# One grid for all the chains of a mixer: writing TensorE's order out by hand

## The chip, the core and the metric

The kernel runs on one core of a Trainium2 chip. The metric is device time in microseconds (us) of one execution; a few executions are timed and their median is given. The profile is one execution on the same core, taken apart by engine: PE (TensorE, matrix products), DVE (VectorE), ACT (ScalarE), POOL (GpSimd) and SP (the queue that issues the weight loads).

## The reference, cut to what matters

A decoder layer on 256 rows of 2048 columns, all in float32:

```
x = LN1(alpha*x + 0.5*swiglu(x, gate1, up1, down1))
p = x @ w_in                                  # 2048 x 6432
o_attn = diff_attention(p[:, :3072])          # 8 heads, two softmaxes each, causal, ALiBi
o_rwkv = rwkv7(p[:, 3072:])                   # 16 heads of 64, delta-rule state, decay, gate
x = LN2(alpha*x + concat(o_attn, o_rwkv) @ w_out)
x = LN3(alpha*x + 0.5*swiglu(x, gate2, up2, down2))
```

The change touches only the two middle products and what lies between them, the mixer. In rwkv7 a state of 64 x 64 per head runs over the rows; `k` is normalised, `r`, `k` and two products of `k` are scaled by cumulated decays, and a gate closes the output.

## The kernel before, in words

**Products.** Every large product is formed from three rounded terms. A pair of weight tiles (256 rows x 512 columns) is loaded by SP into `raw`; ACT rounds it into `wh` (L143), DVE subtracts to get the rest `wl` (L146), and PE adds `wh*xh`, `wl*xh` and `wh*xl` (L153 to L155). The 256 rows of x are two halves of 128 (`tt` 0 and 1). One *step* is one pair of weight tiles: six products for the first half of the rows, and six for the second half with the pair of two steps earlier, so twelve products of 128 x 512. The rounded halves have five slots in this phase (`NW["mix"]`), so ACT can round a new pair only when PE is through with the pair five steps before it.

**Chains.** Between the products stand chains of small operations. `chan_major` turns the finished block of `p` by PE transposes (`tr`, L584), ACT or DVE copies it to `praw`, and `shift` mixes each of its four parts with the previous row: ACT writes `df` (L590), DVE writes the result (L596). `df` has one buffer. `rwkv_group` makes the decays (L731), normalises `k` (Square L746, a product with `bones` L753), scales, and forms `Q` by products masked on DVE (L789, L792); a loop of 31 steps on DVE inverts the triangles of 32 x 32; then the state runs over four blocks (L890 to L930), and two norms and the gate follow (L945 to L980). `rwkv_values` turns `v` (L701) and forms the bonus (L713). `attn_heads` does two heads at a time. There are two groups of everything: rwkv group 0 and 1 (each eight heads), attention group 0 and 1 (each four heads).

**Who sets the order.** Each chain is a Python generator; `Stream.run_bg` is called after each pair of weight tiles and moves the chains on. Up to the last block of `w_in` they advance by credit: each `yield` names a cost, each step grants 1.6 (`BG`) or 0.5 (`AT`), and the order of all engines' instructions is afterwards set by the scheduler of the tile framework, which also moves PE's small matrix products to where it thinks their inputs are ready. The output product `w_out` has three parts: part 0 (attention group 0 and rwkv group 0, 16 steps), part 1 (attention group 1, 8 steps), part 2 (rwkv group 1, 8 steps). In parts 0 and 1 PE's order is written out by hand (`manual_schedule`): PE executes what the program emits, in that order, and each chain moves one `yield` per step. Before a part starts, `ready` drains the chains that it needs and splits their outputs (`split`, L89 and L90). PSUM banks of the chains: `sm` has two, `pr` one, `at` two, shared with `tr`.

Of the kernel before, what the change touches and what calls it, by code (L numbers as in the profile page):

```python
# [16 lines left out]
P = 128  # L17
# [18 lines left out]
BG = 1.6  # L36
AT = 0.5


def build(tc, A, out):  # L40
# [58 lines left out]
    class Stream:  # L99
        def __init__(self):  # L100
            self.pend = []
            self.tail = []
            self.roles = None
            self.behind = []
            self.acc = {}
            self.bg = []
            self.credit = {}
            self.hooks = {}
            self.step = 0
            self.slot = 0  # L110
            self.even = False
            self.hold = {}

# [157 lines left out]
        def flush(self, lag=0):  # L271
# [9 lines left out]
            while self.pend:  # L281
                self.mm(self.pend.pop(0), 1)

        def spawn(self, gen, rate):
            self.bg.append(gen)
            self.credit[gen] = [0.0, rate]

        def run_bg(self):
            if self.even:
                for g in list(self.bg):  # L290
                    if self.hold.get(g):
                        self.hold[g] -= 1
                        continue
                    while g in self.bg:
                        try:
                            if next(g) != 0:
                                break
                        except StopIteration:
                            self.bg.remove(g)
                return  # L300
            for g in list(self.bg):
                c = self.credit[g]
                c[0] = min(c[0], 0.0) + c[1]
                while c[0] > 0 and g in self.bg:
                    try:
                        cost = next(g)
                    except StopIteration:
                        self.bg.remove(g)
                        break
                    if cost is None:  # L310
                        break
                    c[0] -= cost
# [246 lines left out]
    def mix(mp, pq, C):  # L559
# [17 lines left out]
        def chan_major(acc, tt, widths, dst):  # L577
# [3 lines left out]
            tr = bank("tr", (P, 4, P))  # L581
            o = 0
            for i, w in enumerate(widths):
                T.transpose(tr[:w, i, :], tm[:, o:o + w], ident)  # L584
                o += w
            dst(tr)
# [12 lines left out]
        def lora_done(tt, acc):  # L599
            if tt == 0:  # L600
                pr = hp.tile([P, 4, S + 1], F32, tag="J1", name=nm("praw"))
                V.memset(pr[:, :, 0:1], 0.0)
                lora["raw"] = pr
            pr = lora["raw"]

            def dst(tr):
                c = slice(1 + tt * P, 1 + (tt + 1) * P)
# [3 lines left out]
            chan_major(acc, tt, [P, P, 32], dst)  # L611
            if tt == 1:
# [12 lines left out]
                lora.update(tw=tw, g1=g1, g2=g2)  # L625

# [20 lines left out]
        def rwkv_start(g, prev=None):  # L647
# [5 lines left out]
            stream.spawn(st["gen"], BG)  # L653
            return st

        def rwkv_cols(g, st, parts):
            gr = st["group"]

            def done(tt, acc, i):
                if tt == 0:  # L660
                    pr = hp.tile([P, 4, S + 1], F32, tag="J1" if g == 0 and i == 2 else "H3", name=nm("praw"))
                    V.memset(pr[:, :, 0:1], 0.0)
                    st["raw"] = pr
                pr = st["raw"]
                chan_major(acc, tt, [P] * 4, lambda tr: SC.copy(out=pr[:, :, 1 + tt * P:1 + (tt + 1) * P], in_=tr))
                if tt == 1:
# [4 lines left out]
                    if i == 2:  # L671
                        st["gen2"] = rwkv_values(g, st)
                        stream.spawn(st["gen2"], BG)
# [17 lines left out]
        def rwkv_values(g, st):  # L691
            prev = st["prev"]
            while "rk" not in st or (prev is not None and "chain" not in prev):
                yield None
            vp, vv, rk = st["group"].vp, st["group"].vv, st["rk"]
            SV = hp.tile([P, 4, 4, 2, 64], F32, tag="J1", name=nm("SV"))
            st["SV"] = SV
            for p in range(4):
                ps = bank("pr", (P, 4, P))
# [4 lines left out]
                yield 0.3  # L704
# [3 lines left out]
            SC.copy(out=SV[0:64, :, 3, 1, :], in_=ps[0:64, :, 64:128])  # L708
            yield 0.3
            for hf in range(2):  # L710
                ps = bank("pr", (P, 2, S))
# [3 lines left out]
                yield 0.6  # L715
            st["values"] = True

        def rwkv_group(g, st):
# [7 lines left out]
            for hf in range(2):  # L726
                for k in range(2):
                    ps = bank("pr", (P, 2, S))
                    for i in range(2):
                        c0 = (2 * hf + i) * P  # L730
                        T.matmul(ps[:, i, :], wa[:, c0:c0 + P], lora["tw"][:, k, :], start=True, stop=True)  # L731
                    for i in range(2):
                        p = 2 * hf + i
                        o, x = (tl[:, p, :], ps[:, i, :]) if k == 0 else (av[:, p], ps[:, i, :].rearrange("p (c t) -> p c t", c=4))
                        SC.activation(out=o, in_=x, func=AF.Sigmoid, bias=col(k, g, p))
                    yield 0.6
# [13 lines left out]
            for hf in range(2):  # L750
                ps = bank("pr", (P, 2, S))
# [3 lines left out]
                yield 0.6  # L755
# [38 lines left out]
            rk = t4("lw")  # L794
            for p in range(4):
                V.scalar_tensor_tensor(out=v4(rk)[:, p], in0=rh[:, p], scalar=col(4, g, p), in1=ka[:, p], op0=ALU.mult, op1=ALU.mult)
            st["rk"] = rk
            yield 1.5

            def transposed():  # L800
# [5 lines left out]
                for h in range(2):  # L806
                    for e in range(2):
                        r = slice(64 * e, 64 * e + 64)
                        ps = bank("sm", (P, 8, 64))
                        for i in range(8):  # L810
                            T.transpose(ps[:, i, :], BK[r, 2 * h + i // 4, i % 4, e:e + 2].rearrange("p a t -> p (a t)"), ident[r, r])
                        for p in range(2):
                            SC.copy(out=bt[2 * h + p][:, :, e, :], in_=ps[:, 4 * p:4 * p + 4])
# [28 lines left out]
            while "values" not in st or (g == 1 and "over" not in lora):  # L842
                st["wait"] = True
                yield None
            SV = st["SV"]
# [9 lines left out]
            if g == 1:  # L855
                yield from transposed()
# [19 lines left out]
            yield 0.6  # L876
            if g == 0:
                yield from transposed()
            BT = st["bt"]
            st["cols"] = True  # L880
# [4 lines left out]
            for c in range(4):  # L885
# [6 lines left out]
                V.tensor_copy(out=Rs, in_=ps)  # L892
                yield 0.6
# [6 lines left out]
                SC.copy(out=SV[64:128, :, c, 1, :], in_=ps[64:128])  # L900
                yield 0.6
                if c < 3:
# [14 lines left out]
                    yield 0.6 * (1 - g)  # L917
# [23 lines left out]
            for hf in range(2):  # L941
# [5 lines left out]
                yield 0.6 * (1 - g * (1 - hf))  # L947
# [3 lines left out]
            for hf in range(2):  # L951
# [5 lines left out]
                yield 0.6 * (1 - g * (1 - hf))  # L957
            SC.activation(out=merge(nrm), in_=merge(nrm), func=AF.Exp, scale=-0.5)
            yield 0.6 * (1 - g)
            V.tensor_tensor(out=merge(Yc), in0=merge(Yc), in1=merge(nrm), op=ALU.mult)  # L960
            yield 0.6 * (1 - g)
            for p in range(4):
                V.tensor_scalar(out=Yc[:, p], in0=Yc[:, p], scalar1=col(5, g, p), scalar2=col(6, g, p), op0=ALU.mult, op1=ALU.add)
            yield 0.6 * (1 - g)
            V.tensor_tensor(out=sq, in0=Yc, in1=v4(vv), op=ALU.add)
            yield 0.6 * (1 - g)
            st["gate"] = True
            while g == 0 and "v" not in st.get("next", ()):
                yield None
# [278 lines left out]
```

## Time and profile before

| | us |
|---|---|
| median of 3 runs | 1916.03 (1914.43 to 1919.23) |
| profiled execution, its own time | 1915.6 |
| its span | 1913.8 |
| PE busy | 1883.6 (98%) |
| DVE busy | 1624.6 (85%) |
| ACT busy | 1095.3 (57%) |
| mean granted PE clock | 0.995 |

The page gives busy time per engine, and rows by line; a row of the timeline has start, duration, engine, line and operation, and in brackets how long the engine had been idle before it and who released it. PE's products overlap one another in the records, so the distance of their starts counts, not their durations. A small fp32 product that is no transpose leaves two records (64 instructions at L862, 128 records). The mixer lies between about 700 and 1221 us: the first products with `w_in` overlap the end of LN1, `w_out` starts at 1078 us, and LN2 ends it.

### The profile page before, as it was taken

Reading aid. Unit: us, or ns where it says so; the run is one execution under the profiler, and the core shown is the slowest. Engines: PE = TensorE matmul, PEld = TensorE weight load, DVE = VectorE, ACT = ScalarE, POOL = GpSimd, SP = SyncE. Lnnn points to the kernel's source line nnn. Section 1 sums busy time; section 2 is a strip of 40 time slices with the busy share of each in tenths; the row PEclk is TensorE's granted clock in tenths of the full one; section 3 lists DMA queues with packets and bytes.
Section 4 is the critical chain, followed back from the end, with each engine's and each line's share of the span. In section 5 each row is a group of like instructions: output and inputs, shape, how many; then the busy total and the mean of one; then the engine's idle time right before and its main releaser. Section 6 shows DMA issues by size and latency. Waiting matters only on the chain.

```text
span 1913.8 us, 24938 instructions
## 1 busy us (share of the span) xinstructions
PE 1883.6 (98%) x9335; PEld 1549.8 (81%) x9335; DVE 1624.6 (85%) x1834; ACT 1095.3 (57%) x1376; POOL 72.6 (4%) x110
## 2 busy tenths in 40 slices
PE   9999999999999999999999999999999999999997
PEld 7888888888888888887778778788888888888886
DVE  8999987789999976777678777999999778999996
ACT  6656665556666536656555544566666545666651
POOL 0000101100000000000000000000000110000000
PEclk9999999999999999999999999999999999999999
DMA  9766676766667456555445545776666676666743
GB/s 312 247 198 218 186 239 217 233 212 199 217 216 233 142 173 198 163 160 154 146 117 159 162 148 194 260 246 198 199 211 227 213 236 213 197 210 213 228 153 131
DMA packets 207320, 381.72 MB, mean 199 GB/s; under 512 B 23530, under 2 KB 25648, under 8 KB 206944
## 3 DMA queue, kind: packets, MB, share of 16 engines
q1 hardware_dynamic: 182928, 350.53, 56.5%
q0 software_dynamic: 6832, 15.32, 2.9%
q10 hardware_dynamic: 17440, 14.29, 2.6%
q8 instruction: 73, 1.20, 0.3%
q14 instruction: 47, 0.39, 0.1%
HBM read 368.29 MB, written 11.80 MB: 199 GB/s over the span
## 4 chain that ended last, share of the span: by engine, by line
PE 59%; DVE 2%; issue 1%; ACT 1%; DMA 0%; ACTq 0%; DVEq 0%
PE acc L153 18%; PE acc L154 18%; PE acc L155 18%; PE sm L789 1%; DVE wl L146 1%; PE tr L584 0%; PE tr L443 0%; PE at L1027 0%; DVE y L345 0%; PE pr L731 0%; DVE y L353 0%; PE sm L890 0%; PE sm L898 0%; DMA dY<-Y 0%; PE sm L923 0%
## 5 line engine op out<-in xcount | busy, mean ns | idle before, releaser
L143 ACT CAST wh<-raw 128x1024 fp32r<-128x1024 f32 (+2 forms) x833 | 853.7, 1049 | 604.5 <-PE acc L155 377.8
L146 DVE TENSOR_TENSOR wl<-raw,wh 128x1024 fp32r<-128x1024 f32 (+2 forms) x833 | 984.5, 1215 | 207.1 <-ACT wh L143 202.7
L154 PE MATMUL acc<-wl,xh 128*128 128x512 f32 (+1 forms) x1552 | 606.2, 392 | 1.9 <-DVE wl L146 1.9
L155 PE MATMUL acc<-wh,xl 128*128 128x512 f32 (+1 forms) x1552 | 604.8, 391 | 1.0 <-DVE xl L90 1.0
L153 PE MATMUL acc<-wh,xh 128*128 128x512 f32 (+1 forms) x1552 | 600.0, 394 | 5.2 <-ACT xh L89 3.3
L153 PEld LDWEIGHTS acc<-wh,xh 128*128 128x128 f32 x1552 | 292.7, 189 | 67.2 <-ACT xh L89 4.9
L155 PEld LDWEIGHTS acc<-wh,xl 128*128 128x128 f32 x1552 | 292.9, 189 | 61.6 <-DVE xl L90 1.7
L154 PEld LDWEIGHTS acc<-wl,xh 128*128 128x128 f32 x1552 | 292.8, 189 | 61.7 <-DVE wl L146 3.5
L224 DVE TENSOR_TENSOR raw<-raw,raw 128x2048 f32<-128x2048 f32 x112 | 256.0, 2286 | 1.1 <-DMA raw<-in_ffn_w_gate_dram 0.5
L154 PE MATMUL acc<-wl,hh 128*128 128x512 f32 x544 | 212.0, 390 | 0.0
L155 PE MATMUL acc<-wh,hh 128*128 128x512 f32 x544 | 211.4, 389 | 0.0
L153 PE MATMUL acc<-wh,hh 128*128 128x512 f32 x544 | 210.9, 390 | 0.0
L153 PE MATMUL acc<-wh,s 128*128 128x512 f32 x448 | 174.9, 390 | 1.0 <-ACT acc L250 1.0
L155 PE MATMUL acc<-wh,s 128*128 128x512 f32 x448 | 174.6, 390 | 0.0
L154 PE MATMUL acc<-wl,s 128*128 128x512 f32 x448 | 174.3, 389 | 0.0
L153 PEld LDWEIGHTS acc<-wh,hh 128*128 128x128 f32 x544 | 102.1, 188 | 21.8 <-ACT wh L143 0.4
L155 PEld LDWEIGHTS acc<-wh,hh 128*128 128x128 f32 x544 | 102.1, 188 | 21.1
L154 PEld LDWEIGHTS acc<-wl,hh 128*128 128x128 f32 x544 | 102.2, 188 | 20.9
L153 PEld LDWEIGHTS acc<-wh,s 128*128 128x128 f32 x448 | 84.1, 188 | 19.1 <-ACT acc L250 1.5
L154 PEld LDWEIGHTS acc<-wl,s 128*128 128x128 f32 x448 | 84.1, 188 | 17.4
L155 PEld LDWEIGHTS acc<-wh,s 128*128 128x128 f32 x448 | 84.1, 188 | 17.4
L237 ACT COPY acc<-acc 128x512 f32<-128x512 f32 x28 | 16.0, 572 | 51.5 <-PE acc L155 47.8
(264 smaller groups left out, 1095.6 us busy)
## 6 DMA issues: line engine op xcount, KB each, us to landing
raw<-in_ffn_w_up_dram SPq DMA_DIRECT2D x176, 512.0 KB, 5.5
raw<-in_ffn_w_down_dram SPq DMA_DIRECT2D x176, 512.0 KB, 5.5
raw<-in_ffn_w_gate_dram SPq DMA_DIRECT2D x175, 512.0 KB, 4.7
raw<-in_w_in_dram SPq DMA_DIRECT2D x96, 512.0 KB, 3.6
raw<-in_w_out_dram SPq DMA_DIRECT2D x32, 512.0 KB, 4.2
sd<-s POOLq DMA_DIRECT2D x16, 256.0 KB, 4.1
s<-sd POOLq DMA_DIRECT2D x16, 256.0 KB, 5.0
xs<-y ACTq DMA_DIRECT2D x16, 256.0 KB, 2.6
```

Of the source, the lines that this page charges most:

```text
L143: SC.copy(out=wh[:, c, :w], in_=raw[:, c, :w])
L146: self.cut = V.tensor_tensor(out=wl[:, c, :w], in0=raw[:, c, :w], in1=wh[:, c, :w].bitcast(F32), op=ALU.subtract).ins
L153: T.matmul(a, hi, wh[:, j, :w], start=first and j == 0, stop=False, skip_group_check=True)
L154: T.matmul(a, hi, wl[:, j, :w], start=False, stop=False, skip_group_check=True)
L155: i = T.matmul(a, lo, wh[:, j, :w], start=False, stop=last and j == 1, skip_group_check=True)
L224: V.tensor_tensor(out=out, in0=x, in1=y, op=ALU.subtract)
L237: SC.copy(out=u, in_=a)
L789: T.matmul(pe[e][:, c, :], BK[r, p, c, e:e + 2].rearrange("p a t -> p (a t)"), AR[r, p, c].rearrange("p a t -> p (a t)"), start=True, stop ...
```

## The change

All of the mixer from the first rwkv block to the end of part 1 of `w_out` is now emitted under `manual_schedule` for PE; the credit is gone, and every chain advances to its next non-zero `yield` once per step. The transposes of `chan_major` are put off by one step (`put`), and what follows from them (`then`) is run directly behind them, in the same call that moves the chains. Many steps are larger: two PSUM banks (`pr` and `sm`) are used in one step, some `yield`s are 0. The last blocks of `w_in` are in another order: attention group 1 now comes before `v` of rwkv group 1, and in attention `q` before `k`. The bonus operand `rk` is made in `rwkv_values`; `transposed` turns three of the four blocks per head instead of four (the last was not used). The core of the diff:

```diff
+        def put(self, f):
+            self.puts.append((self.step, f))
 
         def run_bg(self):
-            if self.even:
-                for g in list(self.bg):
...
+            while self.puts and self.puts[0][0] < self.step:
+                self.puts.pop(0)[1]()
             for g in list(self.bg):
-                c = self.credit[g]
-                c[0] = min(c[0], 0.0) + c[1]
-                while c[0] > 0 and g in self.bg:
+                if self.hold.get(g):
+                    self.hold[g] -= 1
+                    continue
+                while g in self.bg:
                     try:
-                        cost = next(g)
+                        if next(g) != 0:
+                            break
                     except StopIteration:
                         self.bg.remove(g)
-                        break
-                    if cost is None:
-                        break
-                    c[0] -= cost
...
-        def chan_major(acc, tt, widths, dst):
+        def chan_major(acc, tt, widths, dst, then):
             tot = sum(widths)
             tm = mp.tile([P, NB], F32, tag="tm", name=nm("tm"), bufs=2)
             SC.copy(out=tm[:, :tot], in_=acc[:, :tot])
-            tr = bank("tr", (P, 4, P))
...
+            def turn():
+                tr = bank("tr", (P, 4, P))
+                o = 0
+                for i, w in enumerate(widths):
+                    T.transpose(tr[:w, i, :], tm[:, o:o + w], ident)
+                    o += w
+                dst(tr)
+                if tt == 1:
+                    then()
+
+            stream.put(turn)
...
             for hf in range(2):
-                ps = bank("pr", (P, 2, S))
+                ps = bank(("pr", "sm")[hf * (1 - g)], (P, 2, S))
                 for p in range(2):
                     T.matmul(ps[:, p, :], C["bones"], tl[:, 2 * hf + p, :], start=True, stop=True)
                 V.tensor_scalar(out=tl[:, 2 * hf:2 * hf + 2, :], in0=ps, scalar1=1e-24, scalar2=None, op0=ALU.max)
-                yield 0.6
+                yield 0.6 * max(g, hf)
...
+        ordered = ExitStack()
+        ordered.enter_context(tc.manual_schedule(engines={mybir.EngineType.PE}))
         r1 = rwkv_start(0)
         rwkv_cols(0, r1, (1, 0, 2))
         r2 = rwkv_start(1, r1)
         a1 = attn_cols(0)
         rwkv_cols(1, r2, (1, 0))
         attn_values(0, a1)
+        a2 = attn_cols(1)
         rwkv_cols(1, r2, (2,))
-        stream.drain(gens(a1))
-        a2 = attn_cols(1)
         attn_values(1, a2)
         stream.flush()
-        while "wait" not in r2:
-            stream.advance(r2["gen"])
         lora["over"] = True
```

What it does to the order is seen at three places. The first is PE at `k` of rwkv group 0 (`tr` are the transposes of the block, `tl` the squares of `k`, `acc` the large products). Before, the last transposes of the block and, 71 large products later, the first product with `bones`:

```order
L584 MATMUL tr_6221<-ident,tm_6219 128x128 x4
L153 MATMUL acc_6268<-wh_6203,xh_5770 128x512
...
L153 MATMUL acc_6268<-wh_6362,xh_5804 128x512
L753 MATMUL pr_6248<-tl_5972,bones 128x256 x2
L584 MATMUL tr_6376<-ident,tm_6374 128x128 x4
...
L753 MATMUL pr_6252<-tl_5972,bones 128x256 x2
```

Now (the changed file's own line numbers), with twelve large products between:

```order
L575 MATMUL tr_6242<-ident,tm_6221 128x128 x4
L150 MATMUL acc_6182<-wh_6271,xh_5689 128x512
...
L152 MATMUL acc_6235<-wh_6205,xl_5771 128x512
L757 MATMUL pr_6287<-tl_5966,bones 128x256 x2
L757 MATMUL sm_6291<-tl_5966,bones 128x256 x2
L150 MATMUL acc_6182<-wh_6297,xh_5699 128x512
```

The product with `bones` moved from six steps behind the transposes to one, and both halves stand together.

The second is PE at `v` of group 0 (`vv` is the mixed `v`). Before, 167 rows lie between the block's last transposes and the first transposes of `vv`:

```order
L584 MATMUL tr_6722<-ident,tm_6720 128x128 x4
L154 MATMUL acc_6666<-wl_6705,xh_5678 128x512
...
L155 MATMUL acc_7026<-wh_7387,xl_5710 128x512
L701 MATMUL pr_6762<-ident,vv_5970 128x128 x4
L153 MATMUL acc_7026<-wh_7387,xh_5709 128x512
```

Now:

```order
L575 MATMUL tr_6724<-ident,tm_6687 128x128 x4
L705 MATMUL pr_6758<-ident,vv_5964 128x128 x4
L705 MATMUL sm_6765<-ident,vv_5964 128x128 x4
L150 MATMUL acc_6630<-wh_6774,xh_5689 128x512
...
L705 MATMUL pr_6796<-ident,vv_5964 128x128 x4
```

The transposes of `vv` are now PE's next instruction behind the transposes from which `vv` is made.

The third is ACT where `w_in` ends and `w_out` begins (`v` is the last block's copy, `wh` the rounded weights, `s` the softmax of attention group 1). Before:

```order
L143 CAST wh_9238<-raw_9236 128x1024
...
L1037 ACTIVATE s_9030,ssum_9032<-s_9030,mx_9031 128x128 x2
L1037 ACTIVATE s_9030,ssum_9032<-s_9030,mx_9031 128x256 x2
L991 COPY v_8972<-acc_9054 128x512
L143 CAST wh_9282<-raw_9280 128x1024
L143 CAST wh_9337<-raw_9335 128x1024
```

Now:

```order
L140 CAST wh_9301<-raw_9299 128x1024
L140 CAST wh_9361<-raw_9359 128x1024
L996 COPY v_9258<-acc_9048 128x512
L87 CAST xh_9293<-og_8055 128x512
L140 CAST wh_9426<-raw_9424 128x1024
L140 CAST wh_9482<-raw_9480 128x1024
L996 COPY v_9258<-acc_9101 128x512
```

No exponentials of a softmax, and no last copy of `v`, stand ahead of the first four pairs of `w_out` any more.

More of the change, by code (lines that the diff above doesn't have):

```diff
@@ L659, in done, with dst, then @@
             def done(tt, acc, i):
[L660 to L666, printed above, removed]
+                def dst(tr):
+                    if tt == 0:
+                        assert i < 2 or g == 0 or "chain" in st["prev"]
+                        pr = hp.tile([P, 4, S + 1], F32, tag="J1" if i == 2 else "H3", name=nm("praw"))
+                        V.memset(pr[:, :, 0:1], 0.0)
+                        st["raw"] = pr
+                    SC.copy(out=st["raw"][:, :, 1 + tt * P:1 + (tt + 1) * P], in_=tr)
+                def then():
+                    pr = st["raw"]
                     for p in range(4):
@@ L725, in rwkv_group @@
                 yield None
[L726 to L736, printed above, removed]
+            for k in range(2):
+                ps = [bank(t, (P, 2, S)) for t in ("pr", "sm")]
+                for p in range(4):
+                    T.matmul(ps[p // 2][:, p % 2, :], wa[:, p * P:(p + 1) * P], lora["tw"][:, k, :], start=True, stop=True)
+                for p in range(4):
+                    x = ps[p // 2][:, p % 2, :]
+                    o, x = (tl[:, p, :], x) if k == 0 else (av[:, p], x.rearrange("p (c t) -> p c t", c=4))
+                    SC.activation(out=o, in_=x, func=AF.Sigmoid, bias=col(k, g, p))
+                yield 0.6
             for p in range(4):
@@ L793, in rwkv_group @@
                 yield 1.2
[L794 to L798, printed above, removed]
+            st["fed"] = True
             def transposed():
@@ L841, in rwkv_group @@
             nc.scalar.dma_start(out=dYT, in_=U[0:32])
-            while "values" not in st or (g == 1 and "over" not in lora):
-                st["wait"] = True
+            yield 0.6
+            while g == 0 and "values" not in st:
                 yield None
-            SV = st["SV"]
             TT = hp.tile([P, 16, 64], F32, tag=HT["lw"], name=nm("TT"))
@@ L876, in rwkv_group @@
             yield 0.6
+            bt = transposed()
             if g == 0:
-                yield from transposed()
-            BT = st["bt"]
-            st["cols"] = True
+                yield from bt
+            while "turned" not in st or (g == 1 and "over" not in lora):
+                yield None
+            SV = st["SV"]
             Yc = be
```

149 lines of the change are left out of this document (74 added, 75 removed).

## The prediction

> **What bounds the kernel now.** I read the page's busy times first, then the mixer by stages, then the timeline wherever PE stood.
>
> ```profile
> PE 1883.6 (98%) x9335; PEld 1549.8 (81%) x9335; DVE 1624.6 (85%) x1834; ACT 1095.3 (57%) x1376; POOL 72.6 (4%) x110
> PEclk9999999999999999999999999999999999999999
> ```
>
> PE is the bound, at full clock nearly all along. The mixer by stages (us, then busy us of PE, PEld, DVE, ACT, POOL, then the granted clock):
>
> ```profile
> 704.00:716.00 12.00, 9.06 (x54) 8.23 (x53) 11.85 (x21) 4.19 (x9) 0.99 (x1) 0.86 0.67 214
> 716.00:1076.00 360.00, 358.86 (x2129) 291.66 (x2128) 266.62 (x489) 203.55 (x335) 6.50 (x7) 1.00 0.55 158
> 1076.00:1080.00 4.00, 1.40 (x13) 0.77 (x9) 2.63 (x8) 4.00 (x10) 0.00 (x0) 1.00 0.11 16
> 1080.00:1084.00 4.00, 3.93 (x11) 2.94 (x11) 2.29 (x3) 2.07 (x6) 0.00 (x0) 0.61 0.63 183
> 1084.00:1196.00 112.00, 110.27 (x871) 88.21 (x870) 84.07 (x158) 53.50 (x103) 5.71 (x7) 1.00 0.52 171
> 1196.00:1221.00 25.00, 20.31 (x88) 15.60 (x87) 23.83 (x38) 9.05 (x12) 2.01 (x2) 0.86 0.61 190
> ```
>
> In the 360 us that the change orders anew PE is idle for 1.1 us; in the 112 us already ordered by hand, for 1.7; at the join of `w_in` and `w_out`, for 2.6, and then it runs 3.4 us at half clock. The stops at LN1 and LN2 (first and last row) stay. So there is little to win, and the question is what the new order makes PE wait for.
>
> **What it wins.** The join first:
>
> ```profile
> 1077.20 0.56 ACT L991 COPY v<-acc 128x512 f32<-128x512 f32 x1
> 1077.67 2.94 ACT L143 CAST wh<-raw 128x1024 fp32r<-128x1024 f32 x3
> 1078.76 0.50 PE L153 MATMUL acc<-wh,xh 128*128 128x512 f32 x1 [1.87 <-ACT wh L143]
> 1080.07 0.50 PE L154 MATMUL acc<-wl,xh 128*128 128x512 f32 x1 [0.81 <-DVE wl L146]
> 1142.77 0.50 PE L153 MATMUL acc<-wh,xh 128*128 128x512 f32 x1 [1.23 <-ACT xh L89]
> ```
>
> PE waits 1.87 + 0.81 = 2.7 us for weights that ACT rounds behind exponentials and the last copy of `v`. In the new ACT order four pairs stand ahead of that copy, so this stop goes, and with it the half clock (3.4 us at half rate = 1.7). At 1142.77 part 1 waits 1.2 us for an output of attention group 1; that chain now ends five steps before part 1, so this goes too. The two groups' transposes fall from 64 to 48:
>
> ```profile
> 1075.40 1.02 PE L811 MATMUL sm<-ident,BK 64*128 64x64 f32 x16
> 736.96 1.02 PE L731 MATMUL pr<-tw,cum 128*128 128x256 f32 x4
> 737.63 0.58 PE L153 MATMUL acc<-wh,xh 128*128 128x512 f32 x1
> 738.05 0.40 PE L154 MATMUL acc<-wl,xh 128*128 128x512 f32 x1
> ```
>
> Sixteen take 1.0 us. The first large product behind a small fp32 one holds PE for 738.05 - 737.63 = 0.42 us instead of 0.23, and in the new order there are 17 fewer such returns (80 for 97); at 0.1 (behind transposes, 757.35 below: 0.31) to 0.2 each, 2 us. Together -(2.7 + 1.7 + 1.2 + 1.0 + 2) = **-8.6 us**. The idle in the rows above allows no more than some 2 us beyond that.
>
> **What it costs.** A step is twelve large products:
>
> ```profile
> 1071.22 0.39 PE L153 MATMUL acc<-wh,xh 128*128 128x512 f32 x1
> ...
> 1073.94 0.39 PE L153 MATMUL acc<-wh,xh 128*128 128x512 f32 x1
> ```
>
> Twelve spacings are 2.72 us. A chain operation put one step behind its source is free if the way there is shorter than that. The already ordered parts show it for a way of one operation (a copy, then the next product). The `w_in` part has longer ways. Here is `k` of group 0 before, from transposes to Square:
>
> ```profile
> 757.35 0.60 PE L584 MATMUL tr<-ident,tm 128*128 128x128 f32 x4
> 757.99 0.59 ACT L665 COPY praw<-tr 128x512 f32<-128x512 f32 x1 [0.77 <-PE tr L584]
> 758.61 0.51 ACT L590 ACTIVATE df<-praw,vB 128x256 f32<-128x256 f32 x1
> 759.16 0.48 DVE L596 SCALAR_TENSOR_TENSOR BK<-praw,om,df 128x256 f32<-128x256 f32 x1 [0.44 <-ACT df L590]
> 759.38 1.05 ACT L143 CAST wh<-raw 128x1024 fp32r<-128x1024 f32 x1 [0.25 <-PE acc L155]
> 759.68 0.35 DVE L745 TENSOR_SCALAR AR<-BK,vB 128x256 f32<-128x256 f32 x1
> 760.46 1.23 DVE L146 TENSOR_TENSOR wl<-raw,wh 128x1024 fp32r<-128x1024 f32 x1 [0.43 <-ACT wh L143]
> 768.52 1.05 ACT L746 ACTIVATE tl<-AR 128x1024 f32<-128x1024 f32 x1
> 757.71 0.48 PE L153 MATMUL acc<-wh,xh 128*128 128x512 f32 x1
> 758.02 0.39 PE L154 MATMUL acc<-wl,xh 128*128 128x512 f32 x1
> ```
>
> It took 12.2 us, with four weight pairs in between, and PE had 71 products to do meanwhile. Without any weight work the hops are: transposes to copy 0.64, copy to `df` 0.62, `df` to DVE 0.55, DVE to its reader 0.52. `df` has one buffer, so the four parts follow one another:
>
> ```profile
> ACT df L590 <- DVE vv L596: 4.0, 3, 1.8
> ```
>
> Four parts are 4 x 1.07 = 4.3. What PE waits for, place by place; "low" is without any weight work in the way; "high" adds what ACT's and DVE's new order put there (a 1.05 cast whose slot comes free as the transposes start, half of it hidden, and a second one in the middle):
>
> *1. `k`, group 0.* 0.64 + 0.62 + 4.3 + 0.35 + 1.05 = 6.9 us to the Square's end, against 0.36 (transposes, 757.35 to 757.71) + 2.72 = 3.1 of cover: low 3.9, high +1.7 = 5.6. I take 5.0: the new ACT order has both casts.
>
> *2. `r`, group 0.* The same, with one multiplication on DVE at the end (below, 1.16): 0.64 + 0.62 + 4.3 + 1.16 = 6.7, less 3.1: low 3.6, high 5.3, taken 4.7.
>
> *3. `v`, both groups.* No step at all in between: the second bank of transposes needs the second part: 0.64 + 0.62 + 2 x 1.07 = 3.4, less PE's own 2 x 0.36: low 2.7, high 3.5, taken 3.0, twice.
>
> *4. The lora block.* The decay products stand directly behind its transposes:
>
> ```profile
> 728.89 0.49 PE L584 MATMUL tr<-ident,tm 128*128 128x128 f32 x3
> 731.32 0.42 DVE L608 COPY praw<-tr 128x256 f32<-128x256 f32 x1
> 734.50 0.40 ACT L621 ACTIVATE tw<-tw 64x256 f32<-64x256 f32 x1
> 803.09 1.16 DVE L779 TENSOR_TENSOR AR<-AR,cum 128x1024 f32<-128x1024 f32 x1
> ```
>
> Copy 0.64 + 0.47, then 0.55 + 0.52 + 0.40 = 2.6, less 0.3: low 2.3, high 3.1, taken 2.8.
>
> *5. `k`, group 1.* As 1, but PE also has four small groups of the state chain in the cover:
>
> ```profile
> 1140.49 0.68 PE L898 MATMUL sm<-Rs,TT 64*64 64x64 f32 x16
> 1141.10 0.44 PE L1087 MATMUL at<-ident,ot 128*128 128x128 f32 x2
> ```
>
> Four times 0.6 = 2.4: low 6.9 - 5.5 = 1.4; high, with the state's own copies and scalings on DVE and ACT in the way, 4.8; taken 3.0.
>
> *6. `k` of attention group 1:* 0.64 + 0.59 - 0.36: low 0.9, high 1.9 (one cast ahead), taken 1.0. Group 0's is behind a small group of products and costs nothing while that lasts; without it the same 0.9.
>
> *7. Gate of group 0 among the `Q` of group 1.* Both use the two `sm` banks. In DVE's new order the masks of the first `Q` stand behind the whole closing norm, so PE waits for banks. Each mask or gate multiplication is 0.69 (row below); two of them behind products of the same step are the low end, 1.4; two table loads, two passes and four affines of the norm before the first mask give 7; taken 3.5, nearer the low end because I know the order and not the waits.
>
> ```profile
> L792 DVE TENSOR_TENSOR Q<-sm,maskq 128x512 f32<-128x512 f32 x12 | 8.1, 686 | 4.2 <-PE sm L789 4.2
> ```
>
> Sum of the stops: 5.0 + 4.7 + 6.0 + 2.8 + 3.0 + 1.0 + 3.5 = **26.0 us**; low 18.9, high 35.0. `r` of group 1 has two steps and 1.5 us of small products as cover and is taken at nothing; if the norm's Square is ahead of it on ACT, 1 us. Weights do not become late: while PE stands, ACT and DVE fill all five slots.
>
> Each stop of 2 us or more also costs clock. 1.87 + 0.81 us idle at the join, and 2.33 + 0.68 at LN2, were each followed by half clock, a window of 3.4 us, 1.7 us lost; the 1.23 at part 1 was not:
>
> ```profile
> 1201.22 0.66 PE L83 MATMUL at<-ident,y 128*128 128x128 f32 x4 [2.33 <-DVE y L353]
> 1202.55 0.50 PE L153 MATMUL acc<-wh,xh 128*128 128x512 f32 x1 [0.68 <-ACT xh L89]
> ```
>
> Six of the stops (1, 2, 3 twice, 4, 5) are that long; five at 1.7 = **8.5 us**, low two (3.4), high eight windows (13.6). [...]
>
> Net: 26.0 + 8.5 - 8.6 = **+26 us** (low 18.9 + 3.4 - 8.6 = +14, high +40). The profiled execution took 1915.6 us, 0.4 under the median; so **1942 us**, 1930 to 1956 in its own range.
>
> **The rivals.** *A. Long ways are covered, faster.* The hand-ordered 112 us lose 1.7 us, and if the `w_in` part does as well only the gains remain: 1916 - 8.6 = 1907. It speaks for it that ACT is busy for only 203.55 of 360 us. Against it stand the four chained parts: for `k` alone it would take a way of 3.1 us where the rows add up to 6.9. It decides from stops below 9 us in total. 10%.
>
> *B. No change.* Only the two places of `v` and the lora block stop, 8.8 us, without clock loss: 1916. 8%.
>
> *C. Short stops cost no clock.* Only the two stops near 5 us lose a window: 26.0 + 3.4 - 8.6 = +21, 1937. It has the wait of 1.23 at part 1 for it, the join against it. [...] 15%.
>
> *D. DVE becomes the bound.* It is busy for 266.62 of 360 us already. With the triangular loops in its queue between weights and chains, all places at their high end and a second stop of this kind at the loops: 1916 + 40 + 5 = 1961. 15%.
>
> **How the numbers follow.** Forecast 52%, A 10, B 8, C 15, D 15. Faster by over 0.3% (5.7 us, about what a measurement of this kernel can tell from no change) is A, 0.10; within it B, 0.08; slower the rest, 0.82. The range, 1925 to 1961, leaves out A and B and hardly more.
>
> **What would show it.** PE idle between 716 and 1196 us should rise from 5 to over 25 us, in six or seven stops of 2 to 6 us, released by ACT at the first product with `bones`, by DVE at the first `Q` and at the transposes of `vv`, by ACT's Tanh at the decay products; about five half-clock windows inside the mixer; no stop at the join. The forecast is wrong if those products start without a wait, or if the span of the mixer shrinks.

## The result, and the profile after

The changed kernel takes **1975.97 us** (median of 4 runs, 1973.43 to 1978.69) against 1917.12 for the kernel before: a ratio of 1.0308 [1.0287, 1.0329], 59 us slower. The direction was forecast, the size was not: 1942 us, and a range that ends at 1961.

The page of the kernel after, busy times and the granted clock:

```profile
PE 1895.5 (96%) x9319; PEld 1555.2 (79%) x9319; DVE 1624.1 (82%) x1834; ACT 1093.8 (55%) x1376; POOL 75.9 (4%) x110
PE   9999999999999988889888999999999999999997
PEclk9999999999999999999899999999999999999999
```

The same work on DVE and ACT as before, to within 2 us. The mixer by stages (us, then busy us of PE, PEld, DVE, ACT, POOL, the granted clock, and the share and GB/s of the transfers):

```profile
716.00:1136.00 420.00, 370.07 (x2212) 296.28 (x2211) 270.04 (x498) 205.34 (x341) 6.82 (x7) 0.93 0.46 135
1136.00:1256.00 120.00, 117.76 (x792) 95.00 (x791) 86.70 (x160) 57.35 (x111) 5.71 (x7) 1.00 0.52 170
```

All of the loss is in the `w_in` part, which now ends at about 1138 us instead of 1078: 50 us idle, at a clock of 0.93. The `w_out` parts lose 2.2 us, and there is no stop at the join. PE's waits by line (who waited for whom: us in total, times, longest):

```profile
PE pr L757 <- ACT tl L750: 9.9, 2, 5.3
PE pr L705 <- DVE vv L591: 8.5, 2, 6.1
PE sm L793 <- DVE AR L783: 5.3, 1, 5.3
PE sm L890 <- DVE SV L921: 5.2, 1, 5.2
PE at L1100 <- DVE ot L1096: 4.5, 2, 4.2
PE pr L735 <- ACT tw L615: 3.9, 1, 3.9
PE at L1039 <- ACT k L1009: 3.1, 1, 3.1
PE sm L981 <- DVE Q L796: 2.3, 1, 2.3
PE at L1072 <- ACT qq L1009: 1.8, 1, 1.8
```

To add it up I use PE's records and those of the granted clock between the last stop at LN1 and the first at LN2 (a stretch that every kernel here has). *Idle* is time without a product, *clock* is half of PE's busy time at half clock, *work* is the busy time less that.

| kernel | median us | stretch | work | idle | clock |
|---|---|---|---|---|---|
| before | 1917.1 | 488.0 | 478.4 | 6.2 | 3.4 |
| after | 1976.0 | 546.8 | 471.4 | 53.1 | 22.3 |
| w_in ordered by the framework | 1935.0 | 505.6 | 479.4 | 18.0 | 8.2 |
| k, two steps more | 1951.3 | 520.6 | 472.4 | 35.9 | 12.3 |
| four ways, two steps more | 1933.4 | 506.4 | 472.4 | 27.8 | 6.2 |
| needless products at the stops | 1963.2 | 535.0 | 498.8 | 28.4 | 7.8 |
| nine ways | 1924.7 | 497.6 | 472.1 | 18.7 | 6.8 |
| nine ways, no `df` | 1923.6 | 494.1 | 471.7 | 17.3 | 5.1 |

After less before: +46.9 idle, +18.9 clock, -7.0 work, together +58.8. Each order has its own amount of work: 470 to 474 in all kernels of this study with `w_in` ordered by hand (but for the needless products), 478 to 479 where the framework orders it.

### The profile page after: what moved, and what is told of

Its sections match the earlier page's. It is cut to its first block, busy times and chain, and to the rows that moved or that the text cites. A ratio compares the mean times of both kernels' runs of the same rounds, so it can differ in the third digit from the quotient of the medians.

```text
span 1972.9 us, 24903 instructions
## 1 busy us (share of the span) xinstructions
PE 1895.5 (96%) x9319; PEld 1555.2 (79%) x9319; DVE 1624.1 (82%) x1834; ACT 1093.8 (55%) x1376; POOL 75.9 (4%) x110
## 4 chain that ended last, share of the span: by engine, by line
PE 86%; DVE 7%; DMA 3%; ACT 3%; issue 2%; ACTq 0%; SPq 0%; DVEq 0%
PE acc L150 27%; PE acc L152 27%; PE acc L151 27%; DVE wl L143 2%; ACT wh L140 1%; PE tr L432 1%; DMA raw<-in_ffn_w_up_dram 1%; DMA U<-dU 1%; DMA raw<-in_ffn_w_gate_dram 0%; DVE y L342 0%; DMA raw<-in_w_in_dram 0%; DVE y L334 0%; PE sm L793 0%; DMA raw<-in_w_out_dram 0%; DMA dU<-Q 0%
## 5 line engine op out<-in xcount | busy, mean ns | idle before, releaser
L150 PE MATMUL acc<-wh,xh 128*128 128x512 f32 (+1 forms) x1552 | 613.5, 400 | 3.9 <-ACT xh L87 2.2
```

The lines of the kernel that those rows point to most:

```text
L150: T.matmul(a, hi, wh[:, j, :w], start=first and j == 0, stop=False, skip_group_check=True)
```

## The experiments

*After* is the changed kernel. Each ratio is to the kernel before, run beside it, and differences from after are taken from the ratios.

**1. `w_in` ordered by the framework again**

```diff
-        ordered.enter_context(tc.manual_schedule(...PE))   # ahead of the first block
+            if i == 0:                                     # ahead of part 0
+                ordered.enter_context(tc.manual_schedule(...PE))
```

> The hand-written order of TensorE is taken away in the w_in part and kept in the two parts of w_out that had it before; grid, larger steps and block order stay as changed. Theory 1 (the loss of 59 us is made by the fixed place of chain operations one step, 2.7 us, behind sources whose ways through ACT and DVE are longer): the framework puts weight products in front of what waits, PE idle in 716 to 1196 us falls from 52 to under 12 us, time 1908 to 1925 us. Rival (the grid, the larger steps or the order of blocks cost it, whoever orders): 1950 us or more.

1935.02 us, 1.0099 [1.0084, 1.0114]: between the two expectations. Two windows tell why:

```profile
716.00:1068.00 352.00, 351.67 (x2060) 284.61 (x2058) 256.93 (x459) 197.81 (x324) 6.47 (x7) 1.00 0.53 158
1068.00:1106.00 38.00, 22.52 (x235) 16.44 (x233) 19.32 (x52) 14.22 (x39) 0.27 (x1) 0.64 0.30 78
```

With grid, larger steps and block order as changed, but PE's order left to the framework, PE is idle for 0.3 us in 352: up to 1068 us it is the hand-written order that stops PE. The 15 us behind it are another loss, at the join (experiments 8 and 9), so 19 us of the 59 stay.

**2. Two steps more at `k`; 3. at four ways**

```diff
             yield 1.0
+            yield 1.0
+            yield 1.0
             for hf in range(2):          # bones of k
```

(3 has the same two lines also ahead of the transposes of `v`, and, in group 0, of the first `Q` and of the lora products.)

> One edit: the product with bones of k stands three steps behind the transposes of k in place of one, in both groups; all else as changed. Theory 1: the stops of 5.3 us (group 0) and 4.5 us (group 1) at this product go, with their half clock (2.8 and 2.6 us by the records): 12 to 15 us less than the changed kernel, about 1962 us. Rival (DVE or ACT is the bound, so that the wait moves on to the next product): within 4 us of the changed kernel.

> Two steps more at four ways: k and v of both groups, r and the lora block of group 0; all else as changed. Theory 1: the seven stops there (3.9, 5.3, 5.3, 6.1, 4.5 and 2.4 us: 27.5 us) and their seven stretches of half clock (14 us lost) go; what stays are the stops inside the state chain and the attention (some 14 us and 8 us of clock): 1934 to 1942 us. Rival (a busier engine sets the pace): 1960 us or more, with the stops found elsewhere.

2: 1951.26 us, 1.0186 [1.0170, 1.0201]. 23 us less than after, with 12 to 15 expected. The stop of group 1 went and that of group 0 fell to 2.1, but three stops at which the edit was not aimed fell as well: the one of 5.2 in the state (L890) gave way to one of 1.5, and those at L1100 and L1039 shrank to 1.5 and 0.8. 3: 1933.35 us, 1.0092 [1.0077, 1.0107], at the low end of what was expected. Steps alone take away 41 us.

**4. PE kept busy while it waits**

```diff
+        def warm(x, n):
+            for _ in range(n):
+                T.matmul(x, ident, C["smask"][:, :x.shape[1]], start=True, stop=True)
...
+                if hf == 0:
+                    warm(ps[:, 0, :], (9, 7)[g])       # and at seven other places
```

> The waits stay as they are; ahead of eight of the waiting groups of products TensorE does 4 to 10 needless fp32 products of 256 columns (60 in all, some 0.5 us each) into the bank that is overwritten next, so that it is not idle while it waits. Theory 1 (the half clock behind the stops is itself a part of the loss): no half clock at these eight places, 10 to 18 us less than the changed kernel, 1958 to 1966 us. Rival (the half clock costs nothing, since TensorE would wait anyway): within 4 us, or slower by what the needless products overhang.

1963.15 us, 1.0246 [1.0228, 1.0263]: 12 us less, though PE does 27 us of needless products. The stretch around the stop at `k` of group 0, after and here:

```profile
767.00:776.80 9.80, 5.55 (x13) 4.45 (x14) 5.43 (x9) 2.94 (x4) 0.00 (x0) 0.65 0.29 93
```

```profile
767.00:776.80 9.80, 8.35 (x38) 6.80 (x38) 5.52 (x10) 4.70 (x7) 0.00 (x0) 1.00 0.30 98
```

By the table the clock's loss fell from 22.3 to 7.8, while idle and needless products together (55.8) are about the idle of after (53.1). So the half clock was a loss of its own. Three of the eight places kept it; at L1100 the needless products waited for their bank themselves, 4.3 us.

**5. The transfers of U, Y and T issued from POOL; 6. two steps more between U and its loop**

```diff
-            nc.scalar.dma_start(out=U, in_=dU)     # and dU, dY, dYT, TT, YT
+            nc.gpsimd.dma_start(out=U, in_=dU)
```

```diff
             V.memset(Y.rearrange("p a b -> p (a b)")[:, ::33], 1.0)
             yield 0.6
+            yield 0.6
+            yield 0.6
```

> The changed kernel with one edit: the loads and stores of U, Y and T (dU, U, dY, dYT, TT, YT) are issued from POOL, which is nearly idle, and not from ACT. Theory (ACT's in-order queue is held for some 5 us by these issues, and so the first product of attention group 1 waits 3.1 us and another 1.8 us): both stops go with the half clock behind the first: 4 to 8 us less than the changed kernel, 1968 to 1972 us. Rival (the loop's data come later from POOL, and DVE stands longer behind them): not faster, 1974 us or more.

> The changed kernel with one edit: two steps more between the load of U and the loop on Y, in both groups. Theory (DVE, in order, stands 5.4 us for that load with the attention's scaling behind it, which stops TensorE for 4.25 us at the transposes of its output): DVE waits for the load at most 1 us, that stop and its 3.0 us of half clock go: 5 to 9 us less than the changed kernel, 1967 to 1971 us. Rival (the loop is late next, and a product behind it waits as long): within 3 us of the changed kernel.

5: 1973.17 us, 1.0302 [1.0286, 1.0319], no difference from after. ACT was held by these issues, as its rows of after show (ACTq is its issuing):

```profile
1076.78 0.58 ACT L1009 COPY k<-tr 128x512 f32<-128x512 f32 x1
1077.69 2.64 ACTq L848 DMA_DIRECT2D TT<-dY  x4
1080.93 1.94 ACTq L852 DMA_DIRECT2D YT<-dYT  x1
1085.15 0.58 ACT L1009 COPY k<-tr 128x512 f32<-128x512 f32 x1
1085.78 0.48 PE L1039 MATMUL at<-k,qq 64*128 64x256 f32 x1 [3.15 <-ACT k L1009]
```

and without them the stop at L1039 fell from 3.15 to 0.76. But the data came later, and a wait that after does not have took its place:

```profile
PE sm L860 <- DMA YT<-dYT: 7.9, 2, 5.8
```

The stop at L1039 also fell to 0.8 in experiments 2 and 6, which leave the issues on ACT: what counts is where in ACT's queue they fall.

6: 1962.81 us, 1.0243 [1.0228, 1.0258], 12 us less with 5 to 9 expected. DVE's longest wait for U fell from 5.4 to 2.4 (at most 1 was expected), the stop at L1100 only from 4.25 to 3.37 (without half clock behind it), and the stop in the state went, at which the edit was not aimed. The cause that I gave for L1100 is thus shown in part.

**7. What holds `v` of group 0**

Rows of PE, ACT and DVE of after, from the last transposes to those of `vv`:

```profile
836.83 0.60 PE L575 MATMUL tr<-ident,tm 128*128 128x128 f32 x4
838.63 0.51 ACT L585 ACTIVATE df<-praw,vB 128x256 f32<-128x256 f32 x1
838.67 0.68 DVE L743 TENSOR_TENSOR_SCAN qq<-smask,tl 128x256 f32<-128x256 f32 x1
839.75 0.86 DVE L752 TENSOR_SCALAR BK<-BK,vB 128x256 f32<-128x256 f32 x3
841.54 1.21 DVE L143 TENSOR_TENSOR wl<-raw,wh 128x1024 fp32r<-128x1024 f32 x1
842.95 0.47 DVE L591 SCALAR_TENSOR_TENSOR vv<-praw,om,df 128x256 f32<-128x256 f32 x1
843.56 1.08 PE L705 MATMUL pr<-ident,vv 128*128 128x128 f32 x4 [6.14 <-DVE vv L591]
```

`df` is there at 839.1; DVE takes it at 842.95, behind scans of group 1, scalings and passes of the loop. Two kernels clear that queue; the first by program order, the second so that the loop really needs `v`:

```diff
-            while "tw" not in lora:
+            while "tw" not in lora or (prev is not None and "turned" not in prev):
...
+            while g == 0 and "turned" not in st:
+                yield None
```

```diff
-            V.memset(Y, 0.0)
+            if g == 0:                      # Y from v, times zero
+                V.tensor_scalar(out=Y..., in0=vv[0:64], scalar1=0.0, scalar2=None, op0=ALU.mult)
```

> The changed kernel with DVE's queue cleared ahead of v of group 0, its steps unchanged: the lora products and scans of group 1, and the loop on Y of group 0, come only after the transposes of v of group 0. Theory (the stop at these transposes is 6.1 us and not the 3.0 that I worked out, because scans and the loop stand ahead of the shifts of v in DVE's order): the stop falls to 2.7 to 3.8 us. Rival (the way itself is 6 us long, one df buffer and its hops): it stays above 5 us. Time 3 to 9 us under the changed kernel by the theory, if the later loop makes nothing else late.

> As the kernel with DVE's queue meant to be cleared ahead of v of group 0, where the loop on Y still came ahead of the shifts in DVE's order and the stop was 4.85 + 1.56 us. Now the loop cannot: Y of group 0 is made from v (times zero), so DVE has only weights beside the shifts. Theory (queue): the first part of v is no longer held for 2.5 to 3.8 us on DVE and the stop is 2.5 to 3.6 us. Rival (the way): still above 4.5 us. The time may go either way, since the loop and the chain behind it start some 10 us later: 1955 to 1970 us.

The first: 1960.72 us, 1.0233 [1.0220, 1.0246]; the stop only fell to 4.86, because the framework ordered the loop on DVE ahead of the shifts all the same. The second: 1957.53 us, 1.0217 [1.0202, 1.0232], and

```profile
836.37 1.23 DVE L143 TENSOR_TENSOR wl<-raw,wh 128x1024 fp32r<-128x1024 f32 x1 [1.05 <-ACT wh L140]
837.51 0.48 DVE L591 SCALAR_TENSOR_TENSOR vv<-praw,om,df 128x256 f32<-128x256 f32 x1
838.14 0.63 PE L705 MATMUL pr<-ident,vv 128*128 128x128 f32 x4 [2.49 <-DVE vv L591]
```

2.49 + 0.34 us with nothing but weights in the queue: the way is what I had worked out (3.0), the other half of the stop was the queue. Most of the 14 and 17 us that these two kernels gain on after comes from elsewhere, though: the stops at L890 and L1100 went or shrank below 2 us.

The way itself was tested by taking the buffer `df` out:

```diff
-            SC.activation(out=df[:n], in_=praw[:n, i, 0:S], ...)
-            V.scalar_tensor_tensor(out=dst, in0=x1, ..., in1=d, ...)
+            SC.activation(out=dst, in_=x0, ...)
+            V.scalar_tensor_tensor(out=dst, in0=x1, ..., in1=dst, ...)
```

> The changed kernel without the buffer df: ACT writes the scaled half into the result's own place and DVE adds to it there, so that the four parts of k, r and v no longer follow one another through one buffer; steps and order as changed. Theory (the parts' chain of 4 x 1.07 us is in the way as I worked it out): four parts take 1.07 + 3 x 0.55 = 2.7 us instead of 4.3, so the stops at k and r (5.3, 5.3 and 4.5 us) are each 1.6 us shorter, those at v 0.5 us; with little change of the half clock, 5 to 9 us less than the changed kernel, 1967 to 1971 us. Rival (the parts wait for their turn in the queues, not for the buffer): the stops stay within 0.4 us, 1974 us or more.

1964.24 us, 1.0246 [1.0223, 1.0269], 12 us less. The stop at `k` of group 0 fell by 1.3 us (1.6 worked out), those at `r` (5.3 to 2.0) and at `k` of group 1 (4.5 to 1.4) by more; at `v` nothing changed (6.4), since the queue sets it. DVE's weights came late instead, by 2.9 us once.

**Is DVE the bound?** Half of its loops' passes are left out, a change of 14 us of DVE's work:

```diff
+                if j % 2 == 0:
+                    yield 1.0
+                    continue
```

> The changed kernel without every second pass (the even j) of the two triangular loops on DVE, with the same number of steps; what comes of Y is then not the inverse that the reference needs. It takes some 14 us of work from DVE. Theory 1 (places, not DVE's throughput): only the stops that have the loop in their queue shrink, v of group 0 and the transposes of the attention's output: 3 to 15 us less than the changed kernel, over 1960 us. Rival D (DVE is the bound): at least as much as is taken away and every stop that DVE releases shrinks: under 1955 us.

1970.43 us, 1.0282 [1.0268, 1.0295]: 5 us less, and the stops at `v` (6.2) and at L1100 (4.4) did not shrink. So DVE's throughput is not the bound. The first theory fell too, at its two stops: the framework moved later passes forward, and seven of them, longer ones, still stand ahead of the first part of `vv`, where after has eight.

**8. The loss at the join without the hand-written order.** The last chain, of group 1, was thought to start too late; first its block of `v` was put ahead, then its loop was spread over half the steps (and two steps were added ahead of the transposes of the first heads of attention group 1):

```diff
+        rwkv_cols(1, r2, (2,))
         a2 = attn_cols(1)
-        rwkv_cols(1, r2, (2,))
```

```diff
-                if j % 2 == 0:
+                if j % (2 + 2 * g) == 0:
                     yield 1.0
```

> As the kernel without the hand-written order in w_in (1935 us), with one edit: the block of v of group 1 stands ahead of the blocks q and k of attention group 1 instead of behind them. There TensorE was idle for 1 us up to 1068 us and for 15 us between 1068 and 1106, in the transposes of v, the products of T and the second attention group, with nothing beside them. Theory (that tail comes from the order of blocks: the last chain starts at the end of w_in): the stops at the transposes of v go, 1910 to 1922 us. Rival (without the hand-written order the chains are put off whatever the order of blocks): 1930 us or more.

> As the kernel without the hand-written order in w_in and with v of group 1 ahead of attention group 1 (1932 us; it waits 10.6 us for the T of group 1 and 4.0 us for its attention where w_in ends), with two edits: the loop on Y of group 1 is spread over 7 steps and not 15, and each of the first heads of attention group 1 has two steps more ahead of its transposes. Theory (the loop of group 1, which ended at 1082 us, 8 us after w_in, is what TensorE waits for): both stops and their 5 us of half clock go, 1909 to 1918 us, level with the kernel before or below it. Rival (the loop is bound by DVE's other work and not by its steps): the stop at T stays above 5 us, 1925 us or more.

1932.22 us, 1.0083 [1.0068, 1.0098], and 1934.98 us, 1.0098 [1.0083, 1.0113]: in time both theories fell. The first edit did take away the stops at the transposes of `v`, and the second the one at the attention, but PE then stood longer for T. The loop ends at 1082 and 1084 us whatever its steps, and PE waits for it at the end of `w_in`. In the second kernel in one piece:

```profile
PE sm L860 <- DMA YT<-dYT: 16.0, 1, 16.0
```

The loop starts at 1033 and 1035; ahead of it the framework spreads the `Q` of group 1 from 950 to 1025 us between large products. In after they lie between 988 and 1010, in the kernel of nine ways between 962 and 985.

**9. Framework first, hand from 945 us on**

```diff
-        ordered.enter_context(tc.manual_schedule(...PE))   # ahead of the first block
...
+        ordered.enter_context(tc.manual_schedule(...PE))
         attn_values(0, a1)
```

> The hand-written order begins only with the block v of attention group 0, about 945 us; ahead of it the framework orders TensorE; behind it the steps are those of the kernel with more steps (1924.7 us: bones of k of group 1 and v of group 1 two more, the loop on Y of group 1 two behind its load, attention one). Theory (the framework's order loses 1 us up to there, the hand-written one brings the Q of group 1 in time): no stops before 945 us, the loop of group 1 ends by 1060 us, no stop over 3 us at the join; 1910 to 1919 us. Rival (what the framework has put off by 945 us comes late behind it, as at the join before): 1925 us or more.

> The same, with the shifts that have no buffer df (ACT and then DVE in the result's own place), which took 1.3 to 3.2 us off each stop at k and r and 12 us off the changed kernel. Theory: 0 to 4 us less than the same kernel with df, since few of these ways are waited for any more. Rival (DVE's weights come later, as in the kernel with this one edit, where TensorE waited 0.8 + 2.9 us for them): 2 to 5 us more.

1932.71 us, 1.0093 [1.0078, 1.0108], and 1929.72 us, 1.0076 [1.0059, 1.0092]. The first by stages:

```profile
716.00:915.00 199.00, 198.60 (x1125) 162.40 (x1125) 145.34 (x241) 115.77 (x176) 0.95 (x1) 1.00 0.58 169
915.00:945.00 30.00, 18.89 (x249) 15.76 (x248) 17.30 (x29) 10.75 (x15) 0.95 (x1) 0.72 0.14 41
```

The rival held: the `Q` of group 1 came in time (969 to 986) and nothing stood at the join, but 11 us of stops now stood at the handover, in the state of group 0 that the framework had put off. PE's quiet under the framework is partly a debt, paid where its freedom ends. Leaving out `df` brought 3 us more, as expected, but the two intervals overlap.

**10. More steps**

```diff
-            while "tw" not in lora:
+            while "tw" not in lora or (prev is not None and "fed" not in prev):
...
-                            stream.hold[x] = i
+                            stream.hold[x] = i + g
```

(with two steps behind the load of U, one at the end of each head of attention group 0, a third at `k`; then four places more, then without `df`.)

> On top of the kernel with two steps more at four ways (1933 us): a third step at k of group 0, the lora products of group 1 behind the Q of group 0, one step more at the end of each head of attention group 0 and ahead of attention group 1, two steps more between the load of U and the loop on Y. Its stops there are 2.1, 2.1, 2.6 + 3.2 and 2.5 us, with 6.2 us of half clock. Theory 1 (each stop is a way that is longer than its steps, and goes with enough of them): 14 us less, 1917 to 1923 us. Rival (DVE is the bound; the wait moves to the next product): within 5 us of 1933.

> On top of the kernel with more steps at nine ways (1924.7 us, which still has 18 us of stops and some 7 us of half clock in the mixer): one step more behind the scalings with the decays (both groups), two between the end of the state of group 0 and the Q of group 1, one ahead of the transposes of v of group 1 and one inside the second chunk of the state of group 0. Theory 1: the stops of 2.0, 2.1, 1.3 + 1.4 and 1.9 us go, and two stretches of half clock: 8 us less, 1914 to 1919 us, level with the kernel before. Rival (the chain of group 1 becomes late for the end of w_in, where nothing stands beside it): 1922 us or more.

> The kernel with more steps at nine ways (1924.7 us) without the buffer df. Theory: its ways are covered already but for the weights of 785 us and the state of group 0; 1920 to 1925 us. Rival (DVE's work comes in a heap and weights are late): 1927 us or more.

1924.68 us, 1.0044 [1.0027, 1.0061]; 1926.65 us, 1.0062 [1.0050, 1.0074]; 1923.55 us, 1.0045 [1.0028, 1.0063]. The five ways added to the four of experiment 3 brought 9 us where 14 were expected. The next four places brought nothing: the stops ahead of the `Q` and the `v` of group 1 shrank or went, the one for weights at 785 us (2.0) stayed, and others of 1.8, 1.5, 1.8, 1.7 and 2.4 us came; the rival's late chain did not show, since no stop above 0.7 us stands at the join. Without `df` the time is the same within the noise. With 17 us idle left, no kernel of this study beats the one before; I have no run that says whether steps alone could.

## Why the prediction was right or wrong

The prediction has +22 idle (26.0 of stops less 2.7 and 1.2), +6.8 clock (8.5 less 1.7) and -3.0 work, together +26. Measured were +46.9, +18.9 and -7.0, together +59. The 33 us between them are +8 from stops that I listed, +17 from stops elsewhere, +12 of clock and -4 of work.

The mechanism of the forecast was right: ways that are longer than the step that covers them stop PE. **The step that failed is the list of places. The sum let PE stop at seven of them and put every other wait at nothing; the runs show some 17 us of stops elsewhere. The second is the price of a stop in clock, one window of half clock each and five windows in all; there were 16.**

**The gains: right, and one too small.** The join's stop, its half clock and the wait at part 1 are gone. The work fell by 7.0 instead of 3.0, and it is mostly the order that does this, not the transposes left out: with these left out but the framework's order it is 479.4. I had counted fewer returns from small products to large ones at 0.1 to 0.2 us; what else the order saves was not separated.

**The stops that I listed: 34 us for 26.** `k` of group 0 was 5.33 for 5.0, and its rows are the ones that were summed: copy at 763.71, four `df` from 764.32 to 769.19 with one cast in between, Square from 770.13 to 771.19. `r` was 5.26 for 4.7, the gate 2.31 + 0.85 for 3.5, `v` of group 1 2.36 + 0.41 for 3.0. Too small were the lora block (3.88 for 2.8), `k` of group 1 (4.54 for 3.0), attention group 1 (3.15 for 1.0: transfers issued on ACT) and above all `v` of group 0, 6.14 for 3.0. The sum stays within my high end (I gave 35.0; the seven high ends add up to 34.7), but three places passed their own: the lora block (3.1), attention group 1 (1.9) and `v` of group 0 (3.5). My high ends let only weights and the state's own copies stand ahead of a way. In the lora block the rows show two passes over weights on DVE. At `v` experiment 7 shows scans and a loop of other chains. For attention group 1 the rows show ACT's issues, which I left out although the program had them on ACT before.

**The stops that I did not list: some 17 us.** L890 (5.2), L1100 (4.2), L1072 (1.8) and smaller ones. At L890 the state of group 0 waits for `SV`, whose scaling (L921) stands on DVE behind the scalings of group 1's `k`:

```profile
960.03 1.20 DVE L773 TENSOR_TENSOR BK<-BK,tl 64x1024 f32<-64x1024 f32 x1
961.25 1.22 DVE L774 TENSOR_TENSOR BK<-BK,tl 64x1024 f32<-64x1024 f32 x1
962.58 1.20 DVE L778 TENSOR_TENSOR AR<-AR,qq 128x1008 f32<-128x1008 f32 x1
963.70 0.86 DVE L921 TENSOR_TENSOR SV<-St,PC 64x256 f32<-64x256 f32 x2
964.25 1.48 PE L890 MATMUL sm<-SV,Q 128*64 128x64 f32 x16 [5.16 <-DVE SV L921]
```

In experiment 2, with `k` of group 1 two steps later, this scaling stands ahead of them, at 957.02 us, and no stop is left at L890. At L1100 DVE stands for the load of U, with the attention's scaling behind it:

```profile
1021.83 0.20 DVE L834 TENSOR_TENSOR itmp<-U,Y 64x31 f32<-64x31 f32 x1 [5.39 <-DMA U<-dU]
1025.00 0.41 DVE L1083 TENSOR_SCALAR ot<-at 128x256 f32<-128x256 f32 x1
1030.27 0.69 PE L1100 MATMUL at<-ident,ot 128*128 128x128 f32 x2 [4.25 <-DVE ot L1096]
```

By experiment 6 this is a part of that stop, and the rest stays open. L1072 and the smaller ones were not followed up.

DVE's waits for U in the kernel before, and after:

```profile
DVE itmp L834 <- DMA U<-dU: 8.7, 2, 5.1
```

```profile
DVE itmp L834 <- DMA U<-dU: 7.7, 2, 5.4
```

The wait was there before, at about the same length, and PE had no stop above 0.35 us between 800 and 1076 us; as I read it, because the framework could put PE's products behind it elsewhere. I walked the places where the diff had moved a product closer to its source; I should also have walked the waits of DVE and ACT, and asked at each who is queued behind.

**The clock: 22.3 us for 8.5.** I took one window of half clock for a stop of 2 us or more, five in all. There were 16 windows, of 10 stretches: six stretches have two. By the counts of the last section the idle part of a window tells more than the length of a stop. The stop at `k` of group 0, window by window:

```profile
763.14:766.55 3.41, 2.78 (x13) 1.92 (x11) 2.46 (x4) 2.72 (x5) 0.00 (x0) 1.00 0.67 174
766.55:769.96 3.41, 0.00 (x0) 0.00 (x0) 3.02 (x6) 1.37 (x3) 0.00 (x0) 1.00 0.56 164
769.96:773.38 3.42, 2.13 (x5) 1.78 (x6) 1.38 (x3) 1.06 (x1) 0.00 (x0) 0.51 0.34 128
773.38:776.79 3.41, 3.41 (x9) 2.67 (x9) 1.38 (x2) 0.96 (x1) 0.00 (x0) 0.50 0.00 0
```

The window after the idle one runs at half clock; the stop still reaches 1.3 us into it, and so the next is at half clock as well, though PE is busy all through it. My row for this, at the join, had a stop that ended inside one window. At LN2, my other row, I misread the trace before: I gave its stop one window of 3.4 us, and its clock is low for 6.8 us, from 1203.8 to 1210.6.

```profile
1203.00:1206.00 3.00, 1.99 (x8) 1.29 (x8) 3.00 (x5) 0.59 (x1) 0.00 (x0) 0.63 0.57 116
1206.00:1210.00 4.00, 4.00 (x13) 3.23 (x12) 4.00 (x7) 1.53 (x2) 0.00 (x0) 0.50 0.78 239
```

So the second window could have been forecast.

**The rivals.** A (below 9 us of stops) and B (8.8 us, at `v` and the lora block alone) fell with the 34 us at the listed places. C, that short stops cost no clock, fell: stops of 2.3 us were followed by half clock. D came nearest in time (1961). What it said of loops in DVE's queue is what stood ahead of `v` of group 0; that DVE is the bound is not borne out: 14 us less work on DVE brought 5. That weights do not become late held (1.5 us in two places).

## What to carry to other kernels

Before an order is fixed by hand, list every wait of the engines that feed it, not only the operations that the edit moves: a wait that costs nothing while the fed engine may do something else can become a stop once it may not (here DVE's for U, 5.1 us long without a stop on PE above 0.35, then 5.4 with one of 4.25 behind it). A way through an in-order engine is as long as its own rows plus whatever the scheduler puts ahead of it there, transfers issued on that engine among them; at `v` program order alone took 1.3 us off a stop of 6.1, a real dependency 3.7. And a quiet stretch under a scheduler can be a debt (in experiment 9, 0.4 us idle in 199 and then 11 in 30): look at the place where its freedom ends.

## What was not expected of the hardware

In these runs the half clock went with the idle share of a window. Laid on the grid of 3.41 us that the clock's records show, between 700 and 1300 us of the 19 profiled kernels: of the windows at full clock with under 1.2 us idle, 0 of 2940 were followed by one at half clock; from 1.2 to 1.8 us, 14 of 77; from 1.8 us on, a little over half a window, 102 of 103. A window at half clock was followed by another in 80 of 85 cases where 0.5 us or more of it were idle, and in 6 of 117 where less was. In before and after alone the counts are 0 of 300, 2 of 5 and 10 of 10, then 8 of 8 and 0 of 14. In these two every border of the clock's records lies a whole number of windows behind the first (in before at 712.28 us and 1, 108, 109, 144, 146 and 350 windows later), whatever PE did in between, so the same stop can cost clock or none by where it falls. The stop of 1.51 + 0.67 us at LN1 was followed by a window of half clock in the kernel before; in after, where a border between two windows falls between its two parts, it was not. In the kernel of nine ways a stop of 2.08 us lies across two windows, and the clock stays at 1.00:

```profile
927.54:930.96 3.42, 2.10 (x12) 1.52 (x10) 3.39 (x5) 1.74 (x3) 0.00 (x0) 1.00 0.53 156
930.96:934.37 3.41, 2.59 (x50) 2.23 (x51) 3.41 (x6) 0.89 (x3) 0.00 (x0) 1.00 0.18 28
934.37:937.78 3.41, 3.41 (x29) 2.58 (x28) 2.49 (x7) 1.99 (x5) 0.00 (x0) 1.00 0.86 276
```
